# A decoder trunk on one core: the second half's norm moved between the first K and V products, pools that wait tile by tile, and two MLP groups as seven block products

## The chip, the cores and the metric

The kernel runs on one core of a Trainium2 chip. The metric is the device time of one execution in microseconds, median of several runs; lower is better. A core has TensorE (PE in the profile; PEld is its weight load), VectorE (DVE), ScalarE (ACT), GpSimd (POOL) and SyncE (SP), which here only issues transfers. Each engine works through its own instructions in order and waits on semaphores for the others. Before the change the median is 2509.57 us (2506.57 to 2510.95 in 3 runs).

## The reference

Two layers on a sequence of 1024 tokens, model width 1024. Layer 0 mixes with a diagonal state-space layer (S5), layer 1 with stick-breaking attention; each ends in a squared-ReLU MLP of width 4096. Every sub-layer reads an RMS-normalised, shifted and scaled copy of the residual stream x; shifts, scales and gates come from a conditioning vector c.

```
x = x + g_a * mix0(...)                      # S5 and its gated output product
h = modulate(rms_norm(x, g), shift, scale)
x = x + g_m * (relu(h @ w1[0])**2 @ w2[0])   # first MLP
hkv = modulate(rms_norm(x), ...); k, v = split(hkv @ w_kv); k = rms_norm per head
q = rms_norm per head (modulate(rms_norm(x), ...) @ w_q)
A[t,s] = sigmoid(z[t,s]) * prod over s<j<t of (1 - sigmoid(z[t,j]))
x = x + g_a * (A @ v) @ w_o
x = x + g_m * (relu(h @ w1[1])**2 @ w2[1])   # second MLP
```

All in float32; the kernel writes each float32 operand as a high and a low part and takes three products (hi*hi, hi*lo, lo*hi).

## The kernel before

Everything is kept transposed: x is 8 tiles k of 128 features by 1024 tokens, and the tokens are two halves h of 512. A tile of x is 128x512. `mm3` issues the three matmuls of a product.

A planner (the tile framework's scheduler) orders the instructions of each engine by program order, readiness and its own timing model, and sets the semaphores. `keep_in_program_order` pins an instruction behind what was traced before it on its engine; `ordered_pe` does that for TensorE in attention. Tiles come from pools; a pool that is opened on the bytes of closed pools makes all its tiles wait for every user of those (the default). SP issues nearly all loads and stores, in order. Three raw tiles of 128x1024 are shared by all weight loads and by `gemv`, the product of a weight block with a row, which VectorE does in one reduction (L174).

**The MLP** (`mlp`, L890 to L1055) goes through 8 groups c of 512 hidden features, 4 blocks j each. `ups(c, j)` forms relu(w1 h)^2 for both token halves and splits it into high and low parts (`halves`). `down(c, o, u, i, h)` multiplies a group's 4 hidden blocks with w2 and adds the result, times the gate, to x. In program order group c+1's first up block stands before group c's down products, and its other three (2, 1, 3) behind them. In the second MLP the groups after the first take `seven` in place of `down`: a 2x2 block product with seven products in place of eight (Strassen's scheme). `enter` forms the sums of hidden blocks for it, on VectorE, and `blocks` the sums of weight blocks, on GpSimd. In the first MLP all 8 groups are plain; the last one runs token half 0 first and then half 1, and `done0` follows each output tile.

**Side jobs.** During the first MLP, `mid()` is called after each of a group's four output pairs and after each of its three later up blocks, 7 times a group, and takes 3 or 4 jobs from a list. A job is a `gemv` (for shifts, scales, gates and bias rows) or a `keep`, which loads half a weight unit through GpSimd's queue, scales it, splits it and stores both parts to memory for attention; GpSimd does all of it, with one tile `ks` and one `kr`. There are 18 jobs without a keep at first, then two jobs to one keep.

**The border.** `norm1` is the norm that attention reads. Its squares are summed tile by tile (`square`: ScalarE, then an addition on GpSimd, for the last tile on VectorE), the column sums go through TensorE (`rstd`, L827), twelve small VectorE operations make the reciprocal root, TensorE spreads the row over all partitions (`spread`, L843), and `apply` multiplies and splits each tile (L78, L253, L75). Half 0's norm runs among half 1's down products. Half 1's stands behind the last one, ahead of attention in program order. Then the pools of the MLP close and attention's open. Attention starts with 24 steps of K, V and Q products for half 0 of the first pair of heads (`fill_to(24)`: 16 steps of 6 matmuls with 256 columns for K and V, 8 of 3 matmuls with 512 columns for Q), then half 1, then the next pair of heads. `pm` is a PSUM pool of 2 banks for these products; a bank is emptied by bias additions on VectorE (L81, into `kn` and `kT`).

## Time and profile before

| | |
|---|---|
| median of 3 runs | 2509.57 us |
| profiled execution | 2508.75 us, span 2507.0 us |
| TensorE busy | 2342.5 us (93%), 12536 matmuls |
| weight loads busy | 1974.6 us (79%) |
| VectorE busy | 1733.1 us (69%) |
| ScalarE busy | 941.7 us (38%) |
| GpSimd busy | 908.5 us (36%) |
| HBM | 241.23 MB read, 49.48 MB written |
| mean granted TensorE clock | 0.974 of full speed |
| chain that ended last | TensorE 66%, VectorE 16%, transfers 9%, issue 4% |

The profile records one execution. A matmul's end is modelled, so its duration (some 390 ns for 512 columns) overlaps the next one; the pace is read from the starts. Busy time says how full an engine is, not whether the end waits for it; the waits, the timeline and the chain that ended last say that. The stages are: S5 to about 210 us, its gated output product to about 430, the first MLP to 1128, attention to 1788, output product and second MLP to the end.

### The profile page before, as it was taken

The page shows a single profiled execution, that of the slowest core. Times are in us where ns is not written, and L with a number is a line of the kernel's source. Part 1 is how long each engine was busy: PE and PEld are TensorE (multiplying, and loading weights), DVE is VectorE, ACT ScalarE, POOL GpSimd, SP SyncE. Part 2 cuts the span into 40 slices and gives each one's busy share as a digit, 9 for nine tenths or more (in the row PEclk, how much of TensorE's full clock was granted, in tenths as well). Part 3 has the DMA queues.
Part 4 walks back from the last instruction along what each step waited for, and adds up shares of the span by engine and source line. Part 5 has one row for each costly group of instructions (what it writes and reads, how often), then busy time and mean ns, then how long its engine had stood idle before and what let it go on. Part 6 is the DMA issues. An engine that isn't in the chain of part 4 may idle for free.

```text
span 2507.0 us, 33262 instructions
## 1 busy us (share of the span) xinstructions
PE 2342.5 (93%) x12536; PEld 1974.6 (79%) x12536; DVE 1733.1 (69%) x2574; ACT 941.7 (38%) x1710; POOL 908.5 (36%) x963
## 2 busy tenths in 40 slices
PE   3888999999999999997899999998999999999998
PEld 2767787878788888886888888886778888888886
DVE  7997547766655655454677877787583767876787
ACT  4753124211222122132566666665351232223221
POOL 4663343244444445223333332343110322342334
PEclk8899999999999999998999999999999999999999
DMA  4325754655655544232111111126721111111112
GB/s 150 88 77 193 259 186 157 213 205 192 204 196 182 193 175 173 94 119 85 59 56 51 56 64 68 62 100 213 248 87 51 34 51 59 59 43 51 56 54 76
DMA packets 105344, 297.08 MB, mean 119 GB/s; under 512 B 13280, under 2 KB 25568, under 8 KB 105184
## 3 DMA queue, kind: packets, MB, share of 16 engines
q1 hardware_dynamic: 87264, 240.42, 27.9%
q0 software_dynamic: 15360, 50.34, 5.6%
q10 hardware_dynamic: 2560, 4.20, 0.8%
q8 instruction: 99, 1.62, 0.3%
q14 instruction: 61, 0.50, 0.1%
HBM read 241.23 MB, written 49.48 MB: 116 GB/s over the span
## 4 chain that ended last, share of the span: by engine, by line
PE 66%; DVE 16%; DMA 9%; issue 4%; ACT 2%; POOL 0%; SPq 0%; DVEq 0%; ACTq 0%; POOLq 0%
PE pm L247 9%; PE pm L248 9%; PE pm L249 9%; PE pm L70 8%; DMA raw<-in_adaT_dram 7%; PE pa L969 3%; PE pa L971 3%; PE pa L970 3%; PE pa L249 3%; PE pa L247 3%; PE pa L248 3%; PE pt L70 3%; DVE sn L1250 3%; PE po L70 2%; PE z L70 2%
## 5 line engine op out<-in xcount | busy, mean ns | idle before, releaser
L247 PE MATMUL pm<-h,uh 128*128 128x512 f32 x1200 | 469.3, 394 | 23.8 <-issue 13.8
L249 PE MATMUL pm<-h,ul 128*128 128x512 f32 x1200 | 469.9, 392 | 4.6 <-DVE ul L84 4.6
L248 PE MATMUL pm<-h,uh 128*128 128x512 f32 x1200 | 471.2, 393 | 1.0 <-DVE h L93 0.9
L214 ACT CAST uh<-raw 128x1024 fp32r<-128x1024 f32 x130 | 136.6, 1051 | 481.8 <-PE pa L248 153.1
L247 PEld LDWEIGHTS pm<-h,uh 128*128 128x128 f32 x1200 | 227.5, 190 | 74.2 <-issue 14.0
L174 DVE CUSTOM_DVE_ANT_0 raw<-raw,silr 128x1024 f32<-128x1024 f32 x119 | 162.1, 1365 | 174.0 <-DMA raw<-in_adaT_dram 160.1
L84 DVE TENSOR_TENSOR ul<-raw,uh 128x1024 fp32r<-128x1024 f32 (+1 forms) x158 | 192.4, 1218 | 124.5 <-ACT uh L214 101.8
L249 PEld LDWEIGHTS pm<-h,ul 128*128 128x128 f32 x1200 | 227.6, 190 | 53.5 <-DVE ul L84 5.9
L248 PEld LDWEIGHTS pm<-h,uh 128*128 128x128 f32 x1200 | 227.6, 190 | 49.5 <-DVE h L93 2.3
L70 PE MATMUL pm<-uh,h 128*128 128x256 f32 x960 | 223.0, 299 | 0.0
L1250 DVE TENSOR_TENSOR_SCAN sn<-sn 128x768 f32<-128x768 f32 (+7 forms) x128 | 180.5, 1416 | 47.3 <-ACT sn L1245 45.9
L81 POOL TENSOR_TENSOR raw<-raw 128x256 f32<-128x256 f32 x28 | 26.0, 927 | 412.3 <-DVE ul L84 412.3
L70 PEld LDWEIGHTS pm<-uh,h 128*128 128x128 f32 x960 | 169.1, 196 | 0.5
L969 PE MATMUL pa<-f,uh 128*128 128x512 f32 x392 | 153.2, 391 | 3.3 <-ACT f L907 2.6
L247 PE MATMUL pa<-f,uh 128*128 128x512 f32 x396 | 154.4, 390 | 0.0
L248 PE MATMUL pa<-f,uh 128*128 128x512 f32 x396 | 154.1, 389 | 0.0
L249 PE MATMUL pa<-f,ul 128*128 128x512 f32 x396 | 153.8, 389 | 0.0
L970 PE MATMUL pa<-f,uh 128*128 128x512 f32 x392 | 153.1, 391 | 0.0
L971 PE MATMUL pa<-f,ul 128*128 128x512 f32 x392 | 145.9, 390 | 0.0
L70 PE MATMUL pm<-ul,h 128*128 128x256 f32 x480 | 137.9, 287 | 0.0
L78 POOL TENSOR_TENSOR sg<-sg,sn 128x512 f32<-128x512 f32 x64 | 92.9, 1452 | 123.5 <-DVE sn L1250 57.4
L78 POOL TENSOR_TENSOR ks<-ks,scl 128x512 f32<-128x512 f32 x48 | 61.2, 1274 | 196.2 <-DMA ks<-in_wkv_dram 96.7
(363 smaller groups left out, 5370.5 us busy)
## 6 DMA issues: line engine op xcount, KB each, us to landing
raw<-in_w_dram SPq DMA_DIRECT2D x140, 512.0 KB, 3.3
raw<-in_adaT_dram SPq DMA_DIRECT2D x96, 512.0 KB, 4.1
uh<-kh SPq DMA_DIRECT2D x40, 512.0 KB, 4.1
ul<-kl SPq DMA_DIRECT2D x40, 512.0 KB, 4.1
kh<-kr POOLq DMA_DIRECT2D x64, 256.0 KB, 2.4
kl<-ks POOLq DMA_DIRECT2D x64, 256.0 KB, 3.1
raw<-in_wT_dram SPq DMA_DIRECT2D x24, 512.0 KB, 4.5
raw<-in_wglu_dram SPq DMA_DIRECT2D x20, 512.0 KB, 4.2
```

Of the source, the lines that this page charges most:

```text
L70: return lambda *a, **k: tc.keep_in_program_order(f(*a, **k))
L78: eng.tensor_tensor(o, a, b, op=ALU.mult)
L84: eng.tensor_tensor(o, a, b, op=ALU.subtract)
L174: V.tensor_tensor_reduce(raw, raw, row, 1.0, 0.0, op0=ALU.mult, op1=ALU.add, accum_out=bcol)
L214: ACT.copy(uh, raw)
L247: T.matmul(ps, uh[:, sl], hi, start=first, stop=False)
L248: T.matmul(ps, uh[:, sl], lo, start=False, stop=False)
L249: T.matmul(ps, ul[:, sl], hi, start=False, stop=last)
L969: T.matmul(p, uh[:, sl], hi, start=(i == 0), stop=False)
L970: T.matmul(p, uh[:, sl], lo, start=False, stop=False)
L971: T.matmul(p, ul[:, sl], hi, start=False, stop=(i == 1))
L1250: V.tensor_tensor_scan(g[:, s0:], g[:, s0:], g[:, s0:], 1.0, op0=ALU.mult, op1=ALU.bypass)
```

## The change

It has five parts. All pools that are opened anew on old bytes get `reuse_waits="tile"`: each tile then waits only for the users of earlier tiles on its own bytes. Groups 5 and 6 of the first MLP take `seven`. `keep` gets two sets of tiles, and the list of side jobs goes one job to one keep, 4 a step. Half 1 of the residual stream is written by the last group into new tiles (`late`, which attention uses afterwards for its scores), three of its squares stay in tiles of their own and are summed by TensorE in `rstd`. And half 1's norm moves into attention's first 24 steps: column sums before step 3, spread before step 8, one tile's multiplication and split before each of steps 9 to 16, spread over VectorE and GpSimd. Half 0's norm moves one output pair earlier.

```diff
+    def tile_pool(name, bufs=1, **k):
+        return tc.tile_pool(name=name, bufs=bufs, reuse_waits="tile", **k)
...
     def keep(key, src, c, scale=None):
...
-        raw = adap.tile([P, HN], F32, tag="ks", name=nm("ks"), bufs=1)
-        hi = adap.tile([P, HN], F32R, tag="kr", name=nm("kr"), bufs=1)
+        while len(keeps) < 4:
+            keeps.append(fs0.extra((F32, F32R)[len(keeps) % 2]))
+        raw, hi = keeps[0:2] if c == 0 else keeps[2:4]
...
-        def square(self, k, h):
-            if self.acc[h] is None:
+        def square(self, k, h, into=None):
+            if into is not None:
+                ACT.activation(into, self.xs[k][h], AF.Square)
+                if k == 0:
+                    self.acc[h] = into
+                else:
+                    self.late[h].append(into)
+            elif self.acc[h] is None:
...
+            parts = [self.acc[h], *self.late[h]]
             for j in range(4):
-                T.matmul(p[:, j:j + 1], self.acc[h][:, 128 * j:128 * j + 128], ones, start=True, stop=True)
+                for n, t in enumerate(parts):
+                    T.matmul(p[:, j:j + 1], t[:, 128 * j:128 * j + 128], ones, start=(n == 0), stop=(n == len(parts) - 1))
...
+        def apply_in(self, k, h, eng, eng2):
+            x = self.xs[k][h]
+            mul(x, x, self.y[h], eng)
+            self.hs[k][h] = split(x, eng2)
...
-        def tile(self, dt=F32R):
-            a = self.n % 28 < 8
-            self.n += 1
-            return self.pools["ab"[not a]].tile([P, HN], dt, tag="f", name=nm("f"), bufs=8 if a else 20)
+        def tile(self, dt=F32R, wide=False):
+            self.n += wide
+            if wide and (self.n - 1) % 28 >= 20:
+                return self.extra(dt)
+            return self.pools["a"].tile([P, HN], dt, tag="f", name=nm("f"), bufs=20)
+
+        def extra(self, dt):
+            return self.pools["e"].tile([P, HN], dt, tag="e", name=nm("e"), bufs=8)
...
-            stt(xs[o][h], p, mod[:, gm + o:gm + o + 1], xs[o][h], ALU.mult, ALU.add)
+            x = xs[o][h]
+            if layer == 0 and c == 7 and h == 1:
+                x = place(o)
+            stt(x, p, mod[:, gm + o:gm + o + 1], xs[o][h], ALU.mult, ALU.add)
+            xs[o][h] = x
...
         def fast(c):
-            return layer == 1 and c > 0
+            return c > 0 if layer else c in (5, 6)
...
-        fill_to(24)
         ordered_pe[0] = True
+        for n in range(24):
+            begin(n, ppt_tile, lambda: at("o", 2))
+            fill_to(n + 1)
...
-          + [lambda: shift_row(M_SHA1)] + bias_jobs(16, 24) + [kq_gain], 2,
+          + [lambda: shift_row(M_SHA1)] + bias_jobs(16, 24) + [kq_gain], 1,
...
+    def place(k):
+        if k == 0:
+            pump(999)
+            fs.close("b", "e")
+            late.append(late_es.enter_context(tile_pool("late", side="right")))
+        return late_tile("sg")
...
-        norm1.square(k, h)
+        if h == 1 and k in (0, 6, 7):
+            norm1.square(k, h, late_tile("sn")[:, :HN])
+        else:
+            norm1.square(k, h)
         if h == 1:
             if k == 0:
+                norm1.rstd(0)
                 bias_row(ps_ax(), 0)
-            if k == 0:
-                norm1.rstd(0)
-            if k == 2:
+            if k == 1:
                 norm1.spread(0)
-            if 2 <= k < 2 + 8 // 2:
-                norm1.apply(0, 2 * (k - 2), 2 * (k - 2) + 2)
+            if 1 <= k < 5:
+                norm1.apply(0, 2 * (k - 1), 2 * (k - 1) + 2)
...
-        pump((3, 4)[cyc[0] % 2])
+        pump(4)
...
-    norm1.rstd(1)
-    norm1.spread(1)
-    norm1.pool = (1, 4)
-    norm1.apply(1, 0, 8)
-    pump(999)
-    fs.es.close()
+    def begin(n, p, row):
+        if n == 3:
+            norm1.rstd(1, p())
+        elif n == 8:
+            norm1.spread(1, p(), row())
+        elif 9 <= n < 17:
+            k = n - 9
+            norm1.apply_in(k, 1, G if k in (2, 5) else V, G if k in (0, 2, 5) else V)
+    fs.close("a")
```

## Rows read from the trace of the kernel before

**Rows 1.** Stretches of 25 us: length, each engine's busy us (instructions), clock, DMA share, GB/s.
```profile
525.00:550.00 25.00, 21.39 (x83) 17.09 (x82) 15.23 (x19) 6.36 (x10) 10.41 (x13) 0.86 0.53 190
...
625.00:650.00 25.00, 21.41 (x87) 17.06 (x86) 15.70 (x21) 7.07 (x12) 11.04 (x15) 0.93 0.64 214
...
850.00:875.00 25.00, 25.00 (x112) 20.72 (x111) 20.73 (x28) 3.16 (x3) 11.16 (x11) 1.00 0.79 267
...
1000.00:1025.00 25.00, 25.00 (x112) 20.67 (x112) 12.30 (x13) 4.79 (x7) 13.65 (x16) 1.00 0.38 138
...
2075.00:2100.00 25.00, 25.00 (x112) 20.71 (x111) 23.86 (x34) 5.23 (x7) 12.45 (x11) 1.00 0.25 85
```

**Rows 2.** Timeline of TensorE at the border: start, us, engine, line, [idle before, releaser].
```profile
1128.20 0.39 PE L249 MATMUL pa<-f,ul 128*128 128x512 f32 x1
1128.43 0.28 PE L1124 MATMUL pm<-uh,h 128*128 128x256 f32 x1
...
1134.88 0.39 PE L1124 MATMUL pm<-uh,h 128*128 128x256 f32 x1 [1.67 <-ACT h L253]
...
1136.50 0.95 PE L827 MATMUL pa<-single,f 128*128 128x1 f32 x8
1137.31 0.37 PE L1126 MATMUL pm<-uh,h 128*128 128x256 f32 x1
...
1142.11 0.28 PE L1125 MATMUL pm<-ul,h 128*128 128x256 f32 x1
...
1143.07 0.28 PE L1124 MATMUL pm<-uh,h 128*128 128x256 f32 x1
...
1159.75 0.77 PE L247 MATMUL pm<-h,uh 128*128 128x512 f32 x1 [13.83 <-issue]
...
1167.48 0.39 PE L249 MATMUL pm<-h,ul 128*128 128x512 f32 x1
```

**Rows 3.** Timeline of VectorE, then of GpSimd, at the border.
```profile
1145.98 1.29 DVE L78 TENSOR_TENSOR f<-xall,f 128x512 f32<-128x512 f32 x2 [6.15 <-ACT f L845]
...
1148.08 2.33 DVE L78 TENSOR_TENSOR f<-xall,f 128x512 f32<-128x512 f32 x2
...
1156.33 1.46 DVE L75 TENSOR_TENSOR h<-f,h 128x512 fp32r<-128x512 f32 x2
1157.89 0.43 DVE L81 TENSOR_TENSOR kn<-pm,brow 128x256 f32<-128x256 f32 x1
...
1148.00 1.26 POOL L75 TENSOR_TENSOR h<-f,h 128x512 fp32r<-128x512 f32 x1 [14.37 <-ACT h L253]
```

**Rows 4.** The reductions on the page; TensorE's waits (450 to 1110) and VectorE's (450 to 700).
```profile
L174 DVE CUSTOM_DVE_ANT_0 raw<-raw,silr 128x1024 f32<-128x1024 f32 x119 | 162.1, 1365 | 174.0 <-DMA raw<-in_adaT_dram 160.1
...
PE pm L247 <- ACT rb L901: 7.5, 3, 3.6
...
DVE raw L174 <- DMA raw<-in_adaT_dram: 81.4, 42, 4.4
```

**Rows 5.** GpSimd at one kept piece; kept pieces by stretch; GpSimd's waits (450 to 1110).
```profile
608.30 0.54 POOL L227 DMA_DIRECT2D ks<-in_wkv_dram  x1 [2.57 <-DMA kl<-ks]
612.25 1.03 POOL L78 TENSOR_TENSOR ks<-ks,scl 128x512 f32<-128x512 f32 x1 [3.41 <-DMA ks<-in_wkv_dram]
...
619.62 0.54 POOL L227 DMA_DIRECT2D ks<-in_wkv_dram  x1 [2.36 <-DMA kl<-ks]
...
475.00:500.00 25.00, 9.66 (x11) 1.00 0.75 259
...
1025.00:1050.00 25.00, 4.89 (x5) 1.00 0.21 76
...
POOL ks L227 <- DMA kl<-ks: 146.9, 47, 5.8
```

**Rows 6.** Start of the second MLP: SP's loads of x, and the stretch behind.
```profile
1790.02 9.79 SPq L1611 DMA_DIRECT2D x<-xd  x16
...
1800.00:1825.00 25.00, 22.35 (x100) 17.66 (x99) 13.12 (x24) 9.26 (x15) 12.00 (x10) 1.00 0.80 314
```

More of the change, by code (lines that the diff above doesn't have):

```diff
@@ L111, in open_ax @@
         es = ExitStack()
-        pools["ax"] = es.enter_context(tc.tile_pool(name=f"pax{i}", bufs=4 if "pv" in pools else 6, space=PSUM))
+        pools["ax"] = es.enter_context(tile_pool(f"pax{i}", bufs=4 if "pv" in pools else 6, space=PSUM))
         return es
@@ L131, in open_pv @@
         es = ExitStack()
-        pools["pv"] = es.enter_context(tc.tile_pool(name="ppv", bufs=2, space=PSUM))
+        pools["pv"] = es.enter_context(tile_pool("ppv", bufs=2, space=PSUM))
         es.callback(pools.pop, "pv")
@@ L216, in split_unit @@
         return uh, ul
-    kept = {}
+    kept, keeps = {}, []
     def keep(key, src, c, scale=None):
@@ L838, in rstd, with spread @@
             self.y[h] = y
[L840 to L841 removed]
+        def spread(self, h, p=None, row=None):
+            p, y = ps_ax() if p is None else p, self.y[h]
             for j in range(4):
                 T.matmul(p[:, 128 * j:128 * j + 128], y[:, j:j + 1].broadcast_to([P, P]), ident, start=True, stop=True)
[L844 removed]
+            self.y[h] = self.tile("rr", 1) if row is None else row
             ACT.copy(self.y[h], p)
+        def apply_in(self, k, h, eng, eng2):
+            x = self.xs[k][h]
+            mul(x, x, self.y[h], eng)
+            self.hs[k][h] = split(x, eng2)
         def apply(self, h, k0, k1):
@@ L888, in norm_tiles, with mlp @@
         return norm_tile
-    def mlp(layer, xs, hs, norm, fs, mid=None, done=None):
+    def mlp(layer, xs, hs, norm, fs, mid=None, done=None, place=None):
         w1, w2 = A["w1"][layer], A["w2"][layer]
@@ L1587, in mid @@
         cyc[0] += 1
-        pump((3, 4)[cyc[0] % 2])
-    mlp(0, xs, hs, norm, fs, mid=mid, done=done0)
-    norm1.rstd(1)
-    norm1.spread(1)
-    norm1.pool = (1, 4)
-    norm1.apply(1, 0, 8)
-    pump(999)
-    fs.es.close()
+        pump(4)
+    mlp(0, xs, hs, norm, fs, mid=mid, done=done0, place=place)
+    def begin(n, p, row):
[7 more added lines that the diff above has]
+    fs.close("a")
     ax_es.close()
@@ L1603 @@
     norm2 = Norm(None, xs2, hs2, 3, M_SHM1)
-    oh, rest = attention(xn, bias, xd)
+    oh, rest = attention(xn, bias, xd, begin, late_tile)
+    late_es.close()
     us = {NONE: fetch(("o", NONE))}
@@ L1612 @@
     fs = Inner()
-    ctx.enter_context(fs.es)
-    fs.open("a")
-    fs.open("b")
+    for name in "aeb":
+        fs.open(name)
+        ctx.enter_context(fs.es[name])
     norm2.np_ = norm_tiles(fs)
```

69 lines of the change are left out of this document (38 added, 31 removed).

## The prediction

> **What bounds the kernel now.** I first read the stretches of 25 us, which give each engine's busy time by stage. In both MLPs TensorE is full: 25.00 of 25.00 us with 112 matmuls of 512 columns, in the first MLP (1000 to 1025) as in the second one's block-product groups (2075 to 2100) [rows 1]. That is 25.00 / 112 = 0.2232 us for a matmul, and there a matmul less is time less, as long as nothing takes TensorE's place. The exceptions are two stretches of the first MLP with 21.39 and 21.41 us busy [rows 1], which the list of waits explains (below), and the border between the first MLP and attention, for which I read the timeline of TensorE and then of VectorE and GpSimd. TensorE ends the last down product at 1128.43, waits 1.67 us at 1134.88 for the first half's norm, and stands still for 13.83 us before 1159.75 [rows 2]. The page calls that stand "issue"; VectorE's timeline tells what it was: VectorE works through the second half's norm from 1145.98 to 1157.8, and only at 1157.89 adds the bias to the first K product, which empties the PSUM bank that the Q product waits for [rows 3]. The bias addition itself waits, by program text, for every user of the pools that attention's pools replace, the last norm subtraction among them.
>
> **Part 1, seven block products in groups 5 and 6.** A plain group's down products are 8 outputs x 2 halves x 4 blocks x 3 = 192 matmuls; the seven products are 4 x 7 x 2 x 3 = 168. Two groups save 48 matmuls, 48 x 0.2232 = 10.7 us. They add per group 14 hi/lo splits in place of 8, the sums of hidden blocks, the evacuations of mixed products, and on GpSimd the sums and the split of the weight blocks. In the second MLP the same work stands beside a full TensorE, with VectorE at 23.86 and GpSimd at 12.45 us [rows 1], so it costs nothing where no weight-times-row reductions are in the way. Such reductions are in the way here: the side jobs now go one reduction to one kept weight, four jobs to a step. There are 18 first jobs, then 48 pairs, then 33 jobs of reductions alone, 29 of them real (the others are small additions and row copies). A group is 384 x 0.2232 = 85.7 us and has 7 steps of 12.2 us; the lone reductions fall into steps 28.5 to 36.8, which is group 4 and the start of group 5. They take 29 x 1.365 us [rows 4] = 39.6 us of 8.3 steps or 101 us, 9.8 in 25. With a plain stretch's 12.30 (1000 to 1025, no reductions in it) that is 22.1, and in the 850 to 875 stretch VectorE stood at 20.73 with TensorE full [rows 1]. In the last 32 us the hidden blocks of group 5 come on top: 2 x 10 operations and 2 splits less the 8 plain ones, some 14 x 0.65 = 9 us, 7 in 25, so VectorE is asked for 29.1 in 25 and comes 5 us behind. Group 6's first up product lies between (48 x 0.2232 = 10.7 us) and hides it. Taken: 0; if that cover fails, 5 us.
>
> **Part 2, the kept weights and the reductions.** Each kept piece is loaded, scaled, split and stored by GpSimd with one set of tiles; from one load to the next, 608.30 to 619.62, it is 11.3 us, in which GpSimd mostly waits for its load and its store [rows 5]. The 48 pieces run from about 475 to 1030 [rows 5]. Two sets let the load and the store of one lie beside the work of the other, about 11.3 / 2 = 5.7 us a piece if nothing else limits it. GpSimd must be through before the blocks of group 5: counting back from 1128.4 by matmuls (192 + 144 + 192 + 48 + 144 + 192 = 912, 203.6 us) group 5's down products stand at 925, so a piece may take (925 - 475) / 48 = 9.4 us. It fits. The traffic of a piece (0.75 MB) goes from 66 to 132 GB/s; on 190 to 214 GB/s (525 to 550, 625 to 650) that makes 256 to 280, what the 850 to 875 stretch had (267 GB/s, TensorE full) [rows 1]. Between 450 and 700, however, VectorE stood 81.4 us in 42 waits at reductions whose load had not landed, with other work queued behind, and twice a relu tile came so late that TensorE waited 3.6 us (7.5 in all) [rows 4]. Slower loads make that worse, fewer reductions in the middle (2 a step in place of 2.3) make it better. Bounds: -7.5 (all go) to +10 (three more such waits). Taken: +2.
>
> **Part 3, the border.** From 1128.43 to the end of the first K, V and Q products of half 0 (1167.48 + 0.23) it takes 39.3 us [rows 2]. What TensorE has to do there: 96 matmuls of 256 columns at 0.12 us (8 of them between 1142.11 and 1143.07 [rows 2]) = 11.5; 24 x 0.2232 = 5.4; the column sums, now of three tiles (8 records took 0.81 us to the next matmul [rows 2], so 24 take 2.4); the spread 0.8. Sum 20.1 us, so 19.2 us are to be had: the 13.83, the 1.67, and what the first matmuls after the stand cost (the 24 from 1159.75 on took 7.96 us in place of 5.4).
> What is late next, three places. First: the start of K and V needs the first half's norm; it is issued one output pair earlier (12 matmuls, 2.7 us), where 1.67 was missing, but the added column sums wait for the last gain and square: 0 to 2.5 us, taken 1. Second: the spread stands 8 steps (5.8 us) after the start, its small VectorE chain is queued between gains, norm work and bias additions: 0 to 2, taken 1. Third: the second half's multiplications and splits, 11 on VectorE and 5 on GpSimd. After the spread TensorE has 48 x 0.12 + 5.4 = 11.1 us before it needs the first of these tiles and 13.3 us before the last. Run side by side the work takes 11 x 0.65 = 7.1 us (two took 1.29 [rows 3]). Run one after the other it takes 7.1 + 5 x 1.26 = 13.4, with 0.6 for the spread's copy and 2.5 for bias additions and reductions 16.5 us, 3.2 too late. The row at 1148.08, where two multiplications took 2.33 instead of 1.29 beside a GpSimd subtraction [rows 3], lies nearer the second: taken 2. Net gain 19.2 - 4 = 15.2 us. The store of each tile before it is overwritten goes out behind its gain on SP's queue, some 7 us before the first multiplication, and costs nothing unless SP is held up by then. On GpSimd the zeroing of attention's tiles, the V split and the Q splits stand among the five operations; if they come first the third wait grows (rival A).
>
> **Part 4, pools that wait tile by tile.** Beside the border this bears on the start of the second MLP: the 16 loads of x go out at 1790.02, when attention is through, and in 1800 to 1825 TensorE has 22.35 of 25 us [rows 6]. Earlier loads can return 0 to 2.65 us; taken 1.5. At the first border, after the state-space layer, loads are the limit and I take nothing.
>
> **Sum** against the profiled execution's 2508.75 us (span 2507.0 and 1.75 around it; 0.8 below the median of 2509.57): 2508.75 - 10.7 + 2 - 15.2 - 1.5 = 2483.3, so **2483 us**.
>
> **Rivals.**
> A. The wait moves from the pool to the second half's norm: GpSimd does the zeroing and the V and Q splits before its norm operations, and the second K and V products stand some 8 us longer. For it: GpSimd is slower per operation (1.26 against 0.65) and served in order. Against it: after the spread there are over 11 us, and the tiles with GpSimd work are three of eight. Time 2491.
> B. VectorE, in order, stands at reductions more often: 10 us of TensorE waits beyond those taken, or three. For it the 42 waits [rows 4]; against it that they held TensorE only 7.5 us. Time 2493; at its far end, 20 us, 2503.
> C. Slower: GpSimd isn't through with the kept pieces when group 5's blocks, queued behind them, are due. It decides at 9.4 us a piece; each 1 us beyond costs up to 48 us of standing TensorE, so at 9.9 the gain is spent, and at the old 11.3 it would be 48 x 1.9 = 91 us, 2574. For it: pieces and weight loads share the transfers, and GpSimd serves them in order. Against it: of the 11.3 us, 3.41 and 2.36 are waits for the load and the store [rows 5], which a second set covers; 5.5 are its own. The mechanism that could bring it about is GpSimd's issue of transfers: three a piece, each held until a reduction (1.365 us) ends, would be 5.7 + 4.1 = 9.8 us and a time of about 2483 + 48 x 0.4 = 2502. In the trace the issues take 0.54 us [rows 5], whatever VectorE does.
> The Trainium skill, SBUF — State Buffer, section "SBUF: two separate sides", states that GpSimd can't write the descriptors of its own transfers while VectorE holds the port pair that the two share. By that rule the time would be that 2502; the 0.54 us don't show it, but the pieces' transfers now run at twice the rate.
> D. The border's stand stays for another reason (a bank, a load): gain 5 in place of 15.2, 2493.
>
> **How the numbers follow.** Forecast 0.57 (own range 2471 to 2495), A 0.14, B 0.14, D 0.08, C 0.07. Range 2468 to 2501: the low end is the sum with the old waits of the first MLP gone (2 + 7.5), none of the border's 4 us and all of Part 4's 2.65 (2483.3 - 9.5 - 4 - 1.15 = 2468.6); the high end is A and B together (2483.3 + 8 + 10), short of C. About 0.2% (5 us) is what a measurement of this kernel tells from no change. Faster 0.87 (forecast, A, D and most of B), within 0.2% 0.06 (B's far end, D with B), slower 0.07 (C).
>
> **What would show it.** No stand over 2 us between the last down product and the second half's K and V; the first Q product directly behind the V product; group 5's and 6's products with 112 matmuls in 25 us and 1176 + 336 matmuls in the seven-product lines; kept pieces done before 925 us at 5 to 7 us each; x loads of the second MLP before attention's last product. It would be wrong if TensorE's busy share falls in the first MLP, if GpSimd is still at kept pieces after 925, or if the second K product waits for GpSimd.

## The result, and the profile after

The changed kernel is slower, by 0.8%: 2527.41 us median (2525.17 to 2533.65, four runs) against 2508.07 for the kernel before beside it, ratio 1.0084 [1.0068, 1.0100]. The forecast was 2483 us. The profiled execution's span is 2524.0 us, 17.0 more than before.

Five marks that both traces have show where. A "gain" is the VectorE instruction that adds a down product, times the gate, to x. "Start" is TensorE's first wait for an activation tile of the first MLP (445.54 and 448.88), "MLP" goes from there to the last gain of that MLP on VectorE (1130.71, 1155.10), "border" to TensorE's second wait for an `sg` tile in attention (1215.45, 1233.38), "attention" to the first column sum of the second norm (1818.1, 1834.3), "rest" to the last gain (2502.44, 2519.50). In us:

| kernel | start | MLP | border | attention | rest |
|---|---|---|---|---|---|
| before | 445.5 | 685.2 | 84.7 | 602.7 | 684.3 |
| after | 448.9 | 706.2 | 78.3 | 600.9 | 685.2 |

So the border gained 6.5, attention 1.7, and the first MLP, where 48 matmuls fewer run, lost 21.0. Of the 42.6 us between the forecast and the profiled execution (2525.93) 29.7 lie in the first MLP (-8.7 forecast), 8.7 at the border (-15.2 forecast) and 3.3 in the start, where nothing was forecast.

Stretches of 25 us of the kernel after, as in [rows 1]: length, busy us (instructions) of TensorE, its weight loads, VectorE, ScalarE, GpSimd, then clock, DMA share, GB/s.
```profile
525.00:550.00 25.00, 20.89 (x83) 16.72 (x82) 13.59 (x16) 4.17 (x7) 14.69 (x17) 0.86 0.60 207
...
625.00:650.00 25.00, 25.00 (x112) 20.71 (x111) 19.16 (x18) 6.47 (x10) 18.91 (x20) 1.00 0.60 208
...
875.00:900.00 25.00, 18.56 (x89) 15.60 (x89) 12.90 (x20) 3.27 (x4) 0.00 (x0) 0.86 0.45 149
...
950.00:975.00 25.00, 22.49 (x98) 18.00 (x97) 23.76 (x34) 6.46 (x11) 12.32 (x12) 1.00 0.24 87
1000.00:1025.00 25.00, 25.00 (x112) 20.71 (x111) 12.17 (x18) 8.68 (x14) 3.83 (x5) 1.00 0.10 34
```
From 475 to 850 GpSimd's 9 to 14 us in 25 have become 13 to 19 while the kept pieces run, and TensorE falls short in more stretches; to the one that had a mean granted clock of 0.86 before (525 to 550) a second has come (875 to 900). TensorE's waits from 460 to 1125, of which [rows 4] had 7.5 us, and VectorE's from 450 to 700:
```profile
PE pm L251 <- ACT rb L927: 8.9, 4, 4.1
PE pa L251 <- DVE xall L93: 7.3, 4, 3.3
PE pa L251 <- ACT uh L217: 6.4, 1, 6.4
PE pv L251 <- DVE xall L93: 3.7, 3, 2.5
PE pa L999 <- ACT e L933: 2.0, 1, 2.0
...
DVE raw L177 <- DMA raw<-in_adaT_dram: 75.4, 35, 5.6
```
They are 30.5 us in sum now (two small groups are left out here). VectorE's waits at reductions have not grown in sum (75.4 against 81.4), only the longest has (5.6 against 4.4). The 21.0 us of the MLP are thus 23.0 of waits, less 10.7 for the 48 matmuls, and 8.7 more. Most of these are the lower clock behind the waits: 25 us times one minus the granted clock, summed over the stretches from 450 to 1125, is 12.3 us against 5.3 before (an estimate). How such a wait comes about is seen on the timelines of VectorE, SyncE and TensorE:
```profile
605.74 1.21 DVE L84 TENSOR_TENSOR ul<-raw,uh 128x1024 fp32r<-128x1024 f32 x1
606.88 0.74 DVE L93 SCALAR_TENSOR_TENSOR xall<-pa,mod,xall 128x512 f32<-128x512 f32 x1
...
606.98 0.33 SPq L176 DMA_DIRECT2D raw<-in_adaT_dram  x1
...
611.68 1.64 DVE L177 CUSTOM_DVE_ANT_0 raw<-raw,silr 128x1024 f32<-128x1024 f32 x1 [4.07 <-DMA raw<-in_adaT_dram]
...
613.26 0.74 DVE L93 SCALAR_TENSOR_TENSOR xall<-pv,mod,xall 128x512 f32<-128x512 f32 x1
...
614.05 0.59 PE L251 MATMUL pv<-f,uh 128*128 128x512 f32 x1 [2.52 <-DVE xall L93]
```
SP issues the reduction's load at 606.98, just after VectorE's split of 605.74 has freed a raw tile. VectorE stands 4.07 us at the reduction, whose weights have not landed, then takes 1.64 us for it; the gain at 613.26, queued behind, empties the PSUM bank that TensorE needs.

The kept piece, for [rows 5]: two loads in 608.35 to 621.72, 6.7 us a piece, 7.3 with the pair behind it (the next load is issued at 637.56). The last 46 loads go out from 489.5 to 851.2, 8.0 us a piece, and the last store is issued at 859.99, in place of 1033.32.
```profile
608.35 0.54 POOL L231 DMA_DIRECT2D e<-in_wkv_dram  x1 [2.81 <-DMA kl<-e]
...
612.26 1.96 POOL L78 TENSOR_TENSOR e<-e,scl 128x512 f32<-128x512 f32 x1
...
621.72 0.54 POOL L231 DMA_DIRECT2D e<-in_wkv_dram  x1 [1.85 <-DMA kl<-e]
```
The border, for [rows 2] and [rows 3], on TensorE, VectorE and GpSimd:
```profile
1151.38 0.39 PE L253 MATMUL pa<-f,ul 128*128 128x512 f32 x1
1151.61 0.28 PE L70 MATMUL pm<-uh,h 128*128 128x256 f32 x1
...
1155.02 0.35 PE L70 MATMUL pm<-uh,h 128*128 128x256 f32 x1 [1.82 <-DMA uh<-kh]
1156.20 0.38 PE L70 MATMUL pm<-ul,h 128*128 128x256 f32 x1 [0.82 <-DMA ul<-kl]
...
1158.21 5.28 PE L70 MATMUL pt<-single,sn 128*128 128x1 f32 x24 [1.16 <-POOL sn L81]
1163.35 0.56 PE L70 MATMUL pm<-uh,h 128*128 128x256 f32 x1
...
1184.00 0.39 PE L70 MATMUL pm<-uh,h 128*128 128x256 f32 x1 [2.98 <-DVE rs L1138]
...
1170.73 9.21 DVE L78 TENSOR_TENSOR sg<-sg,o 128x512 f32<-128x512 f32 x6
...
1183.53 0.41 DVE L1138 TENSOR_REDUCE rs<-pm 128x4 f32<-128x256 f32 x1
...
1170.83 3.44 POOL L78 TENSOR_TENSOR sg<-sg,o 128x512 f32<-128x512 f32 x2 [7.90 <-issue]
1174.24 5.15 POOL L75 TENSOR_TENSOR h<-sg,h 128x512 fp32r<-128x512 f32 x3
```
The stand of 13.83 us is gone. In its place are 1.82 and 0.82 for the K and V weights, 1.16 for a sum of squares on GpSimd, and 2.98 for a sum on VectorE that empties a bank. Behind the first three waits TensorE's granted clock is 0.50 from 1158 to 1163 and 0.53 from 1163 to 1167.5, the lower of its two levels (1.2 in place of 2.4 GHz).

### The profile page after: what moved, and what is told of

Its sections match the earlier page's. It is cut to its first block, busy times and chain, and to the rows that moved or that the text cites. A ratio compares the mean times of both kernels' runs of the same rounds, so it can differ in the third digit from the quotient of the medians.

```text
span 2524.0 us, 33400 instructions
## 1 busy us (share of the span) xinstructions
PE 2342.2 (93%) x12504; PEld 1970.9 (78%) x12504; DVE 1811.0 (72%) x2654; ACT 950.8 (38%) x1730; POOL 971.2 (38%) x1013
## 5 line engine op out<-in xcount | busy, mean ns | idle before, releaser
L251 PE MATMUL pm<-h,uh 128*128 128x512 f32 x1192 | 465.3, 393 | 16.5 <-ACT rb L927 8.9
L252 PE MATMUL pm<-h,uh 128*128 128x512 f32 x1192 | 466.7, 392 | 1.6 <-DVE h L93 1.6
L217 ACT CAST uh<-raw 128x1024 fp32r<-128x1024 f32 x122 | 128.2, 1051 | 429.5 <-PE pa L252 111.0
L251 PEld LDWEIGHTS pm<-h,uh 128*128 128x128 f32 x1192 | 225.0, 189 | 67.0 <-ACT rb L927 10.6
L84 DVE TENSOR_TENSOR ul<-raw,uh 128x1024 fp32r<-128x1024 f32 (+1 forms) x158 | 200.5, 1269 | 100.1 <-ACT uh L217 75.3
L70 PE MATMUL pm<-uh,h 128*128 128x256 f32 x1024 | 237.0, 299 | 4.8 <-DVE rs L1138 3.0
L70 PEld LDWEIGHTS pm<-uh,h 128*128 128x128 f32 x1024 | 180.5, 197 | 6.0 <-DVE rs L1138 3.4
L70 PE MATMUL pm<-ul,h 128*128 128x256 f32 x512 | 147.9, 289 | 0.8 <-DMA ul<-kl 0.8
L251 PE MATMUL pa<-f,uh 128*128 128x512 f32 x320 | 126.7, 396 | 13.8 <-DVE xall L93 7.3
L93 DVE SCALAR_TENSOR_TENSOR x<-pa,mod,x 128x512 f32<-128x512 f32 x143 | 103.3, 742 | 44.7 <-PE pa L253 30.4
L70 PE MATMUL pm<-h,uh 128*128 128x512 f32 x402 | 132.9, 412 | 0.0
L999 PE MATMUL pa<-f,uh 128*128 128x512 f32 x332 | 129.6, 390 | 1.4 <-DVE x L93 0.7
L1277 ACT ACTIVATE sn<-z,rrr 128x512 f32<-128x512 f32 (+1 forms) x192 | 111.5, 581 | 49.3 <-PE z L70 46.5
L1000 PE MATMUL pa<-f,uh 128*128 128x512 f32 x332 | 129.2, 389 | 0.0
L1001 PE MATMUL pa<-f,ul 128*128 128x512 f32 x332 | 129.2, 389 | 0.0
```

Of the source, the lines that this page charges most:

```text
L70: return lambda *a, **k: tc.keep_in_program_order(f(*a, **k))
L84: eng.tensor_tensor(o, a, b, op=ALU.subtract)
L93: V.scalar_tensor_tensor(o, a, s, b, op0=op0, op1=op1)
L217: ACT.copy(uh, raw)
L251: T.matmul(ps, uh[:, sl], hi, start=first, stop=False)
L252: T.matmul(ps, uh[:, sl], lo, start=False, stop=False)
```

## The experiments

Times are compared by their ratio to the kernel before, timed beside them on the same chip, since chips differ (its medians were 2508 to 2514 us). "Plain" means groups 5 and 6 without the seven products; "one set", that each kept piece uses the same two tiles; "old mix", the side jobs queued and pumped as in the kernel before. The edits, each against the changed kernel:
```
# plain
-            return c > 0 if layer else c in (5, 6)
+            return layer == 1 and c > 0
# one set
-        raw, hi = keeps[0:2] if c == 0 else keeps[2:4]
+        raw, hi = keeps[0:2]
# old mix
-          + [...] + bias_jobs(16, 24) + [kq_gain], 1,
+          + [...] + bias_jobs(16, 24) + [kq_gain], 2,
-        pump(4)
+        pump((3, 4)[cyc[0] % 2])
# vector (border)
-            norm1.apply_in(k, 1, G if k in (2, 5) else V, G if k in (0, 2, 5) else V)
+            norm1.apply_in(k, 1, V, V)
```

All of them, with the stretches defined above from the profiles, and TensorE's waits from 460 to 1125 summed from the list of waits:

| kernel | us | ratio | start | MLP | border | attention | waits |
|---|---|---|---|---|---|---|---|
| e1 plain | 2530.4 | 1.0097 [1.0073, 1.0120] | 446.4 | 712.0 | 78.8 | 602.1 | 29.3 |
| e2 plain, one set | 2506.5 | 0.9987 [0.9972, 1.0002] | 449.7 | 687.1 | 78.8 | 601.1 | 9.9 |
| e3 plain, old mix | 2518.9 | 1.0038 [1.0020, 1.0055] | 447.3 | 698.1 | 79.0 | 599.5 | 15.8 |
| e4 plain, one set, old mix | 2501.3 | 0.9967 [0.9952, 0.9983] | 445.0 | 688.3 | 79.1 | 598.9 | 10.7 |
| g1 as e1, little GpSimd arithmetic | 2512.1 | 1.0006 [0.9992, 1.0021] | 446.4 | 690.9 | 78.3 | 600.4 | 13.0 |
| m4 as e4, more GpSimd arithmetic | 2575.9 | 1.0250 [1.0227, 1.0273] | 486.6 | 714.7 | 80.8 | 601.7 | 32.0 |
| m1 as e1, five raw tiles | 2499.5 | 0.9951 [0.9932, 0.9970] | 448.8 | 678.0 | 78.4 | 600.9 | 2.8 |
| m2 as e4, five raw tiles | 2503.9 | 0.9963 [0.9948, 0.9979] | 453.6 | 677.7 | 78.7 | 602.7 | 3.8 |
| m3 as m2, vector | 2494.2 | 0.9926 [0.9908, 0.9944] | 452.0 | 675.2 | 74.4 | 600.7 | 1.3 |
| e5 seven, old mix | 2520.6 | 1.0041 [1.0023, 1.0058] | 444.6 | 699.9 | 79.1 | 602.7 | 25.0 |
| e6 seven, one set, old mix | 2614.7 | 1.0413 [1.0389, 1.0437] | 446.1 | 794.8 | 79.2 | 602.8 | 120.6 |
| h1 as e5, kept on ScalarE | 2529.2 | 1.0081 [1.0058, 1.0105] | 446.9 | 704.4 | 79.1 | 601.7 | 26.4 |
| h2 as h1, vector | 2522.1 | 1.0047 [1.0029, 1.0066] | 447.5 | 710.4 | 74.8 | 600.9 | 32.5 |
| p1 before, tile-by-tile waits | 2511.3 | 0.9994 [0.9975, 1.0013] | 445.9 | 690.8 | 84.7 | 603.3 | 13.3 |
| b3 as e4, whole-pool waits | 2508.2 | 0.9991 [0.9976, 1.0005] | 449.2 | 688.9 | 78.6 | 600.6 | 10.6 |
| b1 as e4, vector | 2506.0 | 0.9988 [0.9972, 1.0003] | 448.9 | 687.9 | 75.0 | 602.7 | 9.3 |
| o1 change, four raw tiles | 2504.5 | 0.9986 [0.9968, 1.0004] | 455.7 | 673.2 | 78.8 | 601.8 | 7.4 |
| o2 as o1, vector | 2503.1 | 0.9978 [0.9960, 0.9997] | 454.7 | 683.3 | 74.7 | 604.5 | 13.5 |

The stretches come from one profile each. Starts of kernels with the same work there differ by up to 5 us, attention by as much, and the MLP of o1 and o2, which have the same code there, by 10, so a stretch is read to 5 or 10 us, and what a part costs goes by the medians.

**Which part costs (e1 to e4).** The first four take the change apart: seven products, two sets, mix.

> The changed kernel with groups 5 and 6 of the first MLP as plain down products again (48 matmuls more, 10.7 us). In the changed kernel TensorE waits 30.6 us in the first MLP (470 to 1150 us) against 7.5 before, and the lower clock behind these waits costs some 7 us more. Theory 1 (two sets of kept tiles double the kept pieces' traffic, loads of reductions land late, VectorE stands at them with gains and relu squares queued behind): the waits before 870 us stay (some 19 us), those behind may shrink; time 2522 to 2538. Theory 2 (the job mix, four a step and the last third reductions alone): the same here. Theory 3 (the block products themselves make the waits): waits fall to some 8 us, time 2505 to 2512.

> As the first kernel, and one set of kept tiles for both halves of a piece, as before; job mix one to one, four a step. Theory 1: TensorE's waits in the first MLP fall to 5 to 10 us, VectorE's waits for reductions' loads fall, kept pieces take 11 to 12 us each again; time 2500 to 2512. Theory 2: waits stay near 20 us, time 2522 to 2538.

> As the first kernel, with two sets of kept tiles, but the old job list: two jobs to one kept piece, three and four a step. Theory 1: waits stay near 20 us or grow (more reductions beside the faster pieces), time 2522 to 2538. Theory 2: waits fall to 5 to 10 us, time 2500 to 2512.

> As the first kernel, with one set of kept tiles and the old job list: of the change there are left the border, the pools that wait tile by tile, and 20 in place of 28 tiles for hidden values in plain groups. Theories 1 and 2: waits as before, some 8 us, and the border's gain alone, some 5 us: time 2498 to 2507. Theory 4 (the tiles or the pool waits make the stalls): waits near 20 us, time over 2520.

Without the seven products the time stays, so they are not the cause. The second set of tiles costs 2530.4 - 2506.5 = 23.9 us under the new mix and 17.6 under the old; the new mix costs 11.5 with two sets and 5.2 with one. e3 thus lies between the ranges of Theory 1 and Theory 2: both parts cost. How the new mix costs stays open: under the old one (e3) the pieces are not later than in e1 (the last load is issued at 786.6, in e1 at 843.1) and the reductions are longer (1580 ns on average against 1500, from 500 to 800 us), yet TensorE waits 15.8 us in place of 29.3, so the length of the reductions alone doesn't set the loss. What is left with one set and the old mix (border and pools) is 0.33% faster than before.

**By what the second set costs (g1, m4, h1).** In g1 the kept pieces keep their transfers, and GpSimd's arithmetic is cut to 64 of 512 columns. m4 goes the other way from e4: three multiplications more for each piece, on a tile that nothing reads, and no transfer more. h1 loads a piece one job ahead and gives its scale and cast to ScalarE.
```
# g1: mul, cast and subtraction of a piece
-            mul(r3, r3, scale[...].unsqueeze(2).broadcast_to([P, nk, HN // nk]), G)
-        G.tensor_copy(hi, raw)
-        sub(raw, raw, hi, G)
+            mul(raw[:, 0:64], raw[:, 0:64], scale[...].broadcast_to([P, 64]), G)
+        G.tensor_copy(hi[:, 0:64], raw[:, 0:64])
+        sub(raw[:, 0:64], raw[:, 0:64], hi[:, 0:64], G)
# m4: behind the subtraction
+        for _ in range(3):
+            mul(keeps[2], keeps[2], keeps[2], G)
# h1: behind the load of the next piece
-            mul(r3, r3, scale[...], G)
-        G.tensor_copy(hi, raw)
+            for k in range(nk):
+                ACT.activation(raw[:, m * k:m * k + m], raw[:, m * k:m * k + m], AF.Copy, scale=...)
+        ACT.copy(hi, raw)
```

> Two sets of tiles and the new mix as in the changed kernel, plain products in groups 5 and 6, but each kept piece is scaled, cast and subtracted by GpSimd over its first 64 of 512 columns only (the rest of the tiles is zeroed once); its loads and stores stay whole, so the kept weights are not the reference's. Theory port: what the second set costs is GpSimd's arithmetic, which lengthens VectorE's own instructions beside it; then the reductions of 500 to 800 us go back from 1500 ns to 1310 to 1380 ns, TensorE's waits of 450 to 1120 us fall from 29.3 to under 15 us, and the time is 2505 to 2513 us. Theory transfers: what it costs is the kept pieces' loads and stores, which crowd the other weight loads; then the reductions stay near 1500 ns, the waits at 25 us or more, and the time is 2522 to 2531 us.

> One set, old mix, plain products (2501.3 us), with three more multiplications of 128x512 on GpSimd behind each kept piece, on a tile of its own: its arithmetic nearly doubles and no transfer is added. Theory port: VectorE's reductions lengthen from 1310 to 1450 to 1600 ns from 500 to 800 us, TensorE's waits of 460 to 1125 us grow from 10.7 to 18 us or more, 2508 to 2522 us. Rival: GpSimd has idle time for it, what cost with two sets was the pieces' pace of transfers, and the time stays: 2500 to 2505 us.

The reductions from 500 to 800 us, busy us, mean ns, and the idle time before them, in e1, then g1, then m4:
```profile
L177 DVE CUSTOM_DVE_ANT_0 raw<-raw,silr 128x1024 f32<-128x1024 f32 x42 | 63.0, 1500 | 98.7 <-DMA raw<-in_adaT_dram 98.6
```
```profile
L177 DVE CUSTOM_DVE_ANT_0 raw<-raw,silr 128x1024 f32<-128x1024 f32 x45 | 55.4, 1231 | 122.4 <-DMA raw<-in_adaT_dram 122.4
```
```profile
L177 DVE CUSTOM_DVE_ANT_0 raw<-raw,silr 128x1024 f32<-128x1024 f32 x53 | 84.2, 1589 | 76.0 <-DMA raw<-in_adaT_dram 76.0
```
With the arithmetic gone the reduction takes 1231 ns where it took 1500, the waits fall from 29.3 to 13.0 and the MLP from 712.0 to 690.9, with every transfer in place and at a quicker pace (46 pieces at 5.8 us each, 7.9 in e1): the theory of the transfers falls. In m4, where only arithmetic is added, it takes 1589 against 1310 in e4, and the time grows by far more than the 7 to 21 us expected: the last gain of the MLP stands at 1201.3 in place of 1133.3. Of these 68 us 26 lie in the MLP; 42 lie ahead of it, where the kept pieces of the stage before have the added work too and reach into the norm of the MLP. That norm's instructions that write h on VectorE, from 373 to 510 us, in m4, then in e4:
```profile
L93 DVE SCALAR_TENSOR_TENSOR h<-f,mod,h 128x512 fp32r<-128x512 f32 x16 | 24.9, 1584 | 0.1
```
```profile
L93 DVE SCALAR_TENSOR_TENSOR h<-f,mod,h 128x512 fp32r<-128x512 f32 x16 | 11.5, 747 | 0.3
```
They take twice as long, and TensorE waits 17.2 us for them (0.9 in e4). The direction was right, the size was not foreseen. Not every VectorE instruction lengthens: the gains, with one operand in PSUM, take 740 to 744 ns in e2, e1, g1, m1 and m4 alike (500 to 800 us).

> As the changed kernel with the old mix, but a kept piece is loaded one job ahead, and its scale and its cast are made by ScalarE; GpSimd only subtracts and issues the transfers (1.3 us of arithmetic a piece in place of 3.9). Nothing is left out. Theory port: VectorE's instructions get their old lengths back (reductions 1310 to 1400 ns from 500 to 800 us), most of the 17.6 us of the two sets goes, the seven products stay: 2494 to 2503 us. Rival ScalarE: it now has 2 us more a piece in the queue from which the MLP's activations come, TensorE waits for ra and rb instead, 2508 to 2520 us.

h1 has its first part nearly right: reductions take 1414 ns, against 1508 in e5. The time is the rival's, and worse than it said. ScalarE's waits from 460 to 860:
```profile
ACT e L243 <- DMA e<-in_wkv_dram: 83.2, 20, 12.1
...
ACT e L243 <- DMA e<-in_wq_dram: 38.1, 8, 10.6
```
ScalarE, in order, now stands for the kept pieces' loads with the MLP's activations behind, up to 12.1 us.

**Why lengthened instructions end as waits of TensorE (m1, m2).** Five tiles for raw weights in place of three, for reductions and weight loads alike:
```
+        turns["raw"] = turns.get("raw", -1) + 1
+        if "rx" in pools and turns["raw"] % 5 > 2:
+            return pools["rx"].tile([P, 1024], F32, tag="rx", name=nm("rx"), bufs=2)
         return pools["raw"].tile([P, 1024], F32, tag="raw", name=nm("raw"))
...
-            return self.pools["e"].tile([P, HN], dt, tag="e", name=nm("e"), bufs=8)
+            return self.pools["e"].tile([P, HN], dt, tag="e", name=nm("e"), bufs=4 if self is fs0 else 8)
```

> The changed kernel with plain products in groups 5 and 6 (2530.4 us: two sets, new mix), with five tiles for raw weights in place of three during the first MLP (the two more lie where the seven products' halves lay). Theory in order: VectorE stands at reductions whose load was issued late, because SP has no free tile to load into; with two more tiles the loads run further ahead, VectorE's waits for them from 500 to 800 us (about 80 to 120 us with three) fall to under 50 us, TensorE's waits of 460 to 1125 us fall from 29.3 to under 15 us, 2508 to 2518 us. Rival port alone: the lengthened instructions are what makes the MLP's activations late, loads or not; TensorE's waits stay over 22 us, 2522 to 2532 us.

> One set, old mix, plain products (2501.3 us), with five tiles for raw weights in place of three during the first MLP. Theory in order: TensorE's waits there, 10.7 us, fall to 0 to 4 us: 2493 to 2498 us. Rival: those that are left are not of the loads but of VectorE's order of work, nothing changes: 2499 to 2504 us.

m1 is 31 us faster than e1, faster than before and below its theory's range. Two kernels' waits of TensorE, 460 to 1125, first e1, then m1; under m1 its reductions (500 to 800), which stay long (1430 ns on average); then SP's waits for a reduction to free a tile for a weight load (460 to 870), first e1, then m1:
```profile
PE pa L251 <- DVE xall L93: 8.7, 4, 3.3
PE pa L251 <- ACT uh L217: 8.1, 2, 6.4
PE pm L251 <- ACT rb L927: 6.6, 3, 2.7
PE pv L251 <- DVE xall L93: 4.3, 2, 3.1
PE pv L251 <- ACT uh L217: 1.6, 1, 1.6
```
```profile
PE pm L254 <- ACT ra L930: 2.8, 1, 2.8
...
L180 DVE CUSTOM_DVE_ANT_0 rx<-rx,silr 128x1024 f32<-128x1024 f32 x20 | 29.7, 1486 | 37.3 <-DMA rx<-in_adaT_dram 37.3
L180 DVE CUSTOM_DVE_ANT_0 raw<-raw,silr 128x1024 f32<-128x1024 f32 x21 | 28.9, 1376 | 37.9 <-DMA raw<-in_adaT_dram 37.7
```
```profile
SPq L211 <- DVE mod L177: 123.3, 26, 7.1
```
```profile
SPq L214 <- DVE mod L180: 84.3, 21, 6.0
```
VectorE still waits 75 us for loads (98.6 in e1; under 50 was expected), but in the MLP TensorE waits 2.8 us in all. In g1 SP waits 115.1 us for such tiles, so this wait alone does not make the difference between e1 and g1. With five tiles the second set and the new mix cost the MLP nothing: 678.0 us in m1, 677.7 in m2. m2 falls to 3.8 us of waits and 677.7 in the MLP as its theory said, and yet is no faster than e4: it starts the MLP 8.6 us later. The tiles are open in the stage before too; there TensorE's waits from 200 to 458 are 16.5 us in place of 11.3, the longest, 3.6, for a weight tile whose load is late, and its granted clock from 250 to 300 is 0.90 in place of 0.97. That the order in which loads take the tiles causes this is not shown. So the gain was given back in another stage, which the expectation had not looked at.

**The seven products (e5, e6).**

> The changed kernel with the old mix of side jobs: two sets of kept tiles, seven products. The same with plain products took 2518.9 us. Theory GpSimd's work: the kept pieces are through before group 5 needs the tiles, so nothing stands like the 105 us of the kernel with one set; the seven products take 3 to 10 us off: 2509 to 2516 us, with reductions still near 1500 ns. Rival blocks: group 5's halves are late with two sets as well, 2525 us or more.

> The changed kernel with one set of kept tiles and the old mix of side jobs; the border, the pools and the seven products as in the change. Theory two sets: with the load of the side jobs as before, the seven products give a part of their 10.7 us: 3 to 10 us under the same kernel with plain products (2501.3 us), 2491 to 2498 us. Rival blocks: the halves that the seven products need take VectorE in two groups where it is already 9 tenths busy, and the waits eat the 48 matmuls: 2499 to 2504 us.

e5 is where e3 was, between the two ranges: with VectorE late anyway the 48 matmuls give nothing, and TensorE's waits are 25.0 us where e3 has 15.8. Neither expectation of e6 named what it shows, TensorE, then GpSimd and ScalarE:
```profile
1045.15 0.80 PE L999 MATMUL pa<-e,uh 128*128 128x512 f32 x1 [105.18 <-ACT e L933]
...
1042.63 0.54 POOL L239 DMA_DIRECT2D kl<-e  x1
...
1044.48 0.62 ACT L933 CAST e<-rb 128x512 fp32r<-128x512 f32 x1 [106.23 <-DMA kh<-e]
```
Group 5's halves rotate through the tiles that the kept pieces use; with one set these end at 1042.63, and TensorE stands 105 us for them. That is about the price of rival C at the old pace (91 us), but by another path: group 5's first weight blocks, which rival C has queued behind the pieces, are through GpSimd at 939.6, and it is the tiles that are missing. It is also what the second set is needed for.

**The border (p1, b3, b1, h2, m3).**
```
# p1: the kernel before, all re-opened pools
+        return tc.tile_pool(name=name, bufs=bufs, reuse_waits="tile", **k)
# b3: e4 without it
-        return tc.tile_pool(name=name, bufs=bufs, reuse_waits="tile", **k)
+        return tc.tile_pool(name=name, bufs=bufs, **k)
```

> The kernel before with the tile-by-tile waits on its re-opened pools and nothing else. Theory A, the prediction's: the 13.83 us stand of TensorE at the border is the pool's wait for all of its tiles, so it goes with this part alone; the norm of the second half still stands at its old place, so about half of the 19.2 us come, 2496 to 2503 us. Rival: the stand ends with the norm's row, which still has to be made behind the last products, so the place of the norm decides and the waits alone give 0 to 3 us, 2506 to 2511 us.

> One set, old mix, plain products, the norm's new place at the border, but the pools wait for all of their tiles as before. With the tile-by-tile waits too it is 2501.3 us (0.9967 of before); the waits alone gave nothing (0.9994). Theory place: the norm's place decides, so this keeps the gain, 2500 to 2504 us at a before of 2510. Rival both: the late pool and the attention's pools, opened while the last products run, now wait for all tiles of the pools closed before them, and TensorE stands for 5 to 15 us where it did in the kernel before: 2506 to 2515 us.

TensorE's row at the border in p1, then in b3:
```profile
1165.57 0.76 PE L250 MATMUL pm<-h,uh 128*128 128x512 f32 x1 [13.64 <-issue]
```
```profile
1167.09 0.39 PE L70 MATMUL pm<-uh,h 128*128 128x256 f32 x1 [3.06 <-DVE rs L1138]
```
With the waits alone the stand stays, 13.64 us, and the border takes the 84.7 of before; with the norm's place alone it takes 78.6, as with both. At this place the norm decides, as p1's rival and b3's theory said. In the whole time, though, b3 lies in its rival's range: it is equal with before within its interval and e4 is below it, with a start 4.2 us earlier. Whether that is the pools' waits in the stages before the MLP or the spread of starts stays open.

> One set, old mix and plain products (2501.3 us), with the eight multiplications and the eight subtractions of the second half's norm between the K and V products all on VectorE (two and three of them were on GpSimd). Theory port: the six multiplications on VectorE took 9.23 us, 1.54 us each, because GpSimd worked beside them all the time; alone they take 0.65 us each, all sixteen are done in about 10.5 us, TensorE's 3.0 us wait for the sums of squares falls under 1 us: 2496 to 2499 us. Rival: VectorE just has too much to do there, five more instructions add 3.2 us and the wait grows to 5 or 6 us: 2503 to 2506 us.

> The kernel with the kept pieces' scale and cast on ScalarE, and the sixteen instructions of the second half's norm at the border all on VectorE. Theory port: both parts lower the same blocking at two places, the border's part is worth the 2 to 3 us by which TensorE's wait there fell: 2491 to 2501 us, 0 to 4 us under the kernel without the border's part. Rival: what the border gives is given back in the attention behind it (there the one with the border alone was no faster in total): the same time within 2 us, or slower.

> The same with five tiles, and the sixteen instructions of the second half's norm at the border all on VectorE. By the profiles, last product of the MLP to the norm's row took 75.0 us with it and 79.1 us without. Theory port: 2 to 4 us under the same kernel without it, 2489 to 2496 us. Rival: the attention behind it takes the gain back, the same within 2 us.

VectorE's multiplications in b1, and the wait that was 3.00 us in e4 (2.98 after):
```profile
1152.85 4.90 DVE L78 TENSOR_TENSOR sg<-sg,o 128x512 f32<-128x512 f32 x8
...
1163.92 0.39 PE L70 MATMUL pm<-uh,h 128*128 128x256 f32 x1 [0.78 <-ACT kT L1181]
```
Eight take 4.90 us alone, 0.61 each, where six took 9.21 beside GpSimd, 1.54 each. The border falls from about 79 to 74.4 to 75.0 us in each of the four kernels with this edit. In the totals it is clear of noise in m3 alone (9.6 us below m2, more than the border's 4.3). h2 is 7.0 us below h1, but their intervals overlap; b1 is 4.7 us above e4, timed on another chip and with overlapping intervals, and lies at the edge of its rival's range, though the wait fell as its theory said. In its profile the start and the attention are 3.8 us longer each than in e4, which is within the spread of both.

**The change with one tile more (o1, o2).**

> The changed kernel as it is (2527.4 us: two sets, new mix, seven products), with four tiles for raw weights in place of three during the first MLP and nothing else changed. Theory in order: as with five tiles and plain products (2499.5 us), TensorE's waits before group 5 go almost wholly, and the seven products now show their worth of 48 matmuls, 10.7 us less about 4 us of waits in groups 5 and 6: 2490 to 2498 us. Rival one tile too few: with four tiles half of VectorE's waits for loads stay, 2502 to 2515 us. Rival blocks: the seven products take from VectorE in groups 5 and 6 what they give TensorE, 2498 to 2502 us.

> The changed kernel with four tiles for raw weights, and the sixteen instructions of the second half's norm at the border all on VectorE. Theory port: with five tiles the border's part took 9.6 us off the median and 4.3 us off the border's own stretch; here 4 to 10 us under the kernel with four tiles alone: 2483 to 2492 us. Rival: the larger part of the 9.6 us was not the border, and here it is 0 to 3 us.

One more raw tile (the edit of m1 with `% 4` and `bufs=1`, the pool `e` as it was) takes the changed kernel from 1.0084 to 0.9986 [0.9968, 1.0004]. The time is in the range of the rival "one tile too few", and VectorE's waits for loads did stay (77 us from 500 to 800, 101 without the tile); its reductions, at 1601 ns on average, are longer still; but TensorE hardly feels them, 7.4 us, and the MLP is the shortest of all, 673.2. What is missing against the theory is the start, 455.7 (448.9 without the tile). TensorE's longest wait from 225 to 458:
```profile
PE pm L254 <- ACT uh L220: 19.0, 1, 19.0
```
That is the stage before again, waiting for a weight load: ScalarE's cast stands 15.72 us for it, until 271.73. A kernel that opens the extra tile only with the MLP was not tried. o2's border is 4.1 us shorter than o1's, but its median is only 1.4 lower, as its rival said, and in the one profile its MLP is 10 us longer with the same code, so o2 doesn't settle more. The best that ran is m3, 0.9926 [0.9908, 0.9944]: one set, plain products, five raw tiles, border on VectorE.

## Why the prediction was wrong

**Part 2 is the step that failed.** It took +2 us for the first MLP's waits, with +10 as the far bound. The waits grew by 23.0 us (7.5 to 30.5), and in e1, which has no seven products, by 21.8 and the MLP by 26.8. It took GpSimd's arithmetic beside VectorE at nothing, and expected the new mix to help (2 reductions a step in place of 2.3), where it cost 5.2 to 11.5 us. The sum priced the second set by its transfers, "it fits", and looked at reductions and landing times. It left out that GpSimd's arithmetic lengthens VectorE's instructions with two operands in SBUF (g1, m4). The price was in the rows: the prediction used the row in which two multiplications took 2.33 us in place of 1.29 beside GpSimd [rows 3] for the border and not for the MLP. And it left out how thin the cover was: three tiles for raw weights carry both reductions and weight loads, so a VectorE that is late makes SP's loads late too (606.98 in the timeline after; m1). Either cure alone takes the loss away: less arithmetic with three tiles takes 21 us off e1's MLP (0.9% of the time, by the ratios of e1 and g1), long instructions with five tiles 34 (1.5%). That is the mechanism of rival B, VectorE in order with gains behind reductions, with another trigger and just above its far end of 20 us beyond those taken. So the loss needs both; how much each us of lengthening costs, and what the new mix adds to it, stays open.

At the border the serial case was one of the two ends weighed: 13.4 us one after the other. From 1170.73 to the last split, 1183.6, it took 12.9 with two bias additions in it. The six multiplications at 0.61 (b1) and GpSimd's two at 1.03 [rows 5] and three at 1.26 [rows 3] add up to 9.5 us, and the two engines took 9.2 and 8.6 for them side by side: one works while the other stands. The Trainium skill, SBUF — State Buffer, section "SBUF: two separate sides", calls the port pair of the two an exclusive lock, which a VectorE instruction with two SBUF inputs and a GpSimd instruction that reads SBUF hold in turn for their whole length. By that rule the work goes one after the other, and the trace agrees. The rule of the same section that the prediction weighed, on descriptors, which the section states of VectorE instructions in a mode that takes both ports, doesn't show: GpSimd's issues take 0.54 to 0.59 us in the kernel after too (460 to 1125). The pieces' 8.0 us lie midway between the 5.7 of Part 2 and the 9.8 of that rival, but in g1, with every issue in place, they are 5.8, so the arithmetic made the difference.

**Part 3** had the mechanism partly right and the size wrong: 15.2 us expected, 6.5 measured. The stand went, but by the norm's place, not by the pools' waits, by which the prediction explained it: p1 takes these away and the stand stays, since the bias addition stands behind the norm in VectorE's own order. From the last down product to the second K product it is 32.4 us where 20.1 was TensorE's work. The three waits taken at 1 + 1 + 2 came to 1.16, none, and 2.98; not foreseen were the K and V weights (2.64), whose last loads stand on SP's queue behind a store of x that waits for its gain and were issued at 1153.37, 1.8 us behind the start of K (0.3 before), and the clock, which behind these waits was at its lower level: the 24 column sums took 5.14 us to the next matmul in place of 2.4, and the 19 matmuls from 1163.35 to 1167.43 took 4.1 in place of 2.3.

**Part 1**: the 48 matmuls are gone, and of their 10.7 us 4.2 went into waits at 928 to 968 us, 2.0 of them at the first block product. Seven against plain is -5.8 us in the MLP under the new mix (after against e1), +1.9 under the old (e5 against e3), both within the spread of that stretch; in the medians it is -0.13% and +0.03%, nothing clear of noise. The cover priced at 5 us failed in part; 0 had been taken.

**Part 4**: 1.5 us expected. The attention stretch is 1.7 us shorter, but that isn't the mechanism: x is still loaded behind attention's last product (from 1803.86, the product at 1800.88), TensorE's wait for a gain on it is 3.37 us where it was 1.78, and runs with the same attention differ by 5.6 us. The agreement is luck.

**Rivals.** A: no. GpSimd's zeroing did run first, but was through at 1162.9, 7.9 us before its norm operations could start; the V and Q splits came behind them, and the wait was VectorE's. C: refuted in the kernel after, where the pieces end at 860, 65 us before the 925 by which they were due, and by another path seen in e6. D: the stand went, but the gain of 6.5 is nearer D's 5 than the 15.2: of what took its place 2.64 us are loads, 2.98 a bank, as D named them, and some 4.5 the clock.

## What to carry to other kernels

Before work is packed more densely on GpSimd, compare a VectorE instruction's duration in stretches with and without GpSimd's arithmetic beside it; the difference times the number of instructions is a price, on an engine that seemed to have room. Where an in-order engine mixes jobs that wait for loads with jobs that TensorE waits for, count the buffers of the loads first: two raw tiles took 31 us off the kernel with two sets here, and nothing off the median of the one with one set. A saving in a stage is to be read in that stage and then looked for in the next ones: here the gain of more raw tiles was given back in the stage before in m2 and o1.

## What was not expected of the hardware

From 500 to 800 us VectorE's reductions of 128x1024 took 1231 ns on average with little arithmetic on GpSimd (g1), 1310 to 1420 with one set (e4, e2, before, p1), 1485 to 1690 with two (after, e1, e5, e3, o1, o2; 1430 in m1, with five raw tiles), and 1589 with multiplications added (m4), while gains with one operand in PSUM stayed at 740 to 744 ns. GpSimd's own subtraction lengthened too, from 1359 ns (e2) to 1543 (e1). The 24 one-column matmuls of the border, behind three short waits, took 0.21 us each where eight took 0.10 each before [rows 2], at a granted clock of 0.50 from 1158 to 1163.
